# Attention in a one-core kernel: a fourth slot for the keys, the first block's operands loaded by themselves, and projection products ahead of two transposition groups

## The chip, the cores and the metric

The program runs on one core of a Trainium2 chip. A core has a matrix engine (PE in the profile; PEld is its weight load, which runs beside it), a vector engine (DVE), a scalar engine (ACT), a general engine (POOL), and a queue engine (SP) that issues nearly all transfers. The metric is the device time of one execution in microseconds (us), and lower is better.

## The reference, cut to what matters

The program computes a two-layer backbone over 1024 latent tokens with 256 context tokens ahead of them. Only the first layer's mixer, differential attention with 8 heads, is touched here; the second layer and both MLPs are computed as before.

```python
def attend(q, k, v):
    s = jnp.einsum('bqhcd,bkhcd->bhcqk', q, k).astype(jnp.float32)
    p = jax.nn.softmax(s, axis=-1)
    w = p[:, :, 0] - lam * p[:, :, 1]
    o = jnp.einsum('bhqk,bkhe->bqhe', w.astype(v.dtype), v)
    return rmsnorm(o, subln_g) * (1.0 - lambda_init)
...
q_l, k_l, v_l = jnp.split(jnp.einsum('btd,de->bte', h_lat, w_qkv), [QK_COLS, 2 * QK_COLS], axis=-1)
q_l = apply_rope(heads_qk(q_l), cos, sin) * scale
k_l = apply_rope(heads_qk(k_l), cos, sin)
```

A head has two score maps (c = 0 and 1) over 1280 keys, and its result is the first softmax less lambda times the second, times the values. Latent queries see all 1280 keys, and context queries the 256 context keys.

## The kernel before, in words

**Precision and products.** A float32 operand is held as a rounded high part and a remainder. `mm3` (L130) makes one product of three matmuls, which are the lines L132, L133 and L134 of the profile, so whole projections show up as runs of these three lines. Score matmuls are L575 (unit 0) and L581 (other units).

**Two stages.** `phase_v` (L360) normalises the tokens, computes the values of all heads and stores them in DRAM (Vd). In the last token blocks of its loop (`nb` 1, `n` from 1) it also runs `b_start` (L652), a generator that computes head 0's keys and queries, one projection group at each `n`: three for the keys, then three for the queries. Each group is scaled or rotated on ACT, DVE and POOL, split into its two parts in the 4 KB tile `self.stg` (kilobytes 12 to 16 of the region R), and stored from there to Kd or Qd. Then `phase_b` (L679) does the attention.

**Units.** `phase_b` runs 72 units, nine for each head, and then five that only finish. Unit 0 of a head (u0) has the context queries and needs only the first 256 columns of the two key maps; units u1 to u8 have 128 latent queries each against all keys. In a unit n the engines do:

- PE: the scores of this unit; where there are any, the weights-times-values products of an earlier pair of units; then three parts, each made of the transpositions of the previous unit's weight matrix (L622, L627: 4, 2 and 4 blocks of 128 x 128) and some of the eight products of a projection group for the next head. `AHEAD` says which unit has which group, and `FILLS` how the eight products are dealt to the parts: without an entry three, three and two, each behind its part's transpositions.
- DVE: `maxima` copies both score maps out of PSUM while it takes their extremes (L594), `combine` subtracts the maps (L612, L613, L615), L636 makes the low part of the first transposed part, and L529, L524, L537 and L138 serve the projection groups.
- ACT: L635 and L640 take the transposed parts out of PSUM, L604 is the exp of a score map (two in a unit), and L137 and L528 serve the groups.
- POOL: L641 and L642 split the second and third transposed part, L534 is the sine product of the rotation.

The first and the third transposed part share PSUM bank 5 in units that have a group. In the units 0, 1 and 4, 6, 8 ("late") L636 comes behind `combine` on DVE, so the first transposed part of the following unit waits for it.

**What sets the order.** In `phase_b` PE, DVE, ACT and POOL run in the order in which the code is written. SP's order is made by a scheduler, which puts a transfer where its model of the program finds it ready, and SP issues strictly in that order. A transfer that has to wait for something holds up all behind it on SP. All these transfers share one queue (q1).

**Slots.** K of a head is two tiles of 1280 columns (c = 0 and 1) in three slots of the region R1 (5 KB each, `Kr`, L687), so the second key map of the next head goes into a slot that the current head still reads, and is loaded after unit 8's scores (`load_k` behind `scores`). For head 7 it goes to the start of R. Q has two slots of 256 queries (`Qr`), V four (`Vr`). Head 0's first loads are `load_k` twice, `load_q` twice and `load_v`, at the start of `phase_b` (L853 to L857).

Of the kernel before, what the change touches and what calls it, by code (L numbers as in the profile page):

```python
# [6 lines left out]
F32 = mybir.dt.float32  # L7
F32R = mybir.dt.float32r
# [5 lines left out]
KB = 256  # L14
# [47 lines left out]
class Ring:  # L62
# [3 lines left out]
    def next(self):  # L66
        self.i += 1
        return self.items[self.i % len(self.items)]


class Prog:
# [288 lines left out]
    def phase_v(self):  # L360
# [7 lines left out]
        wr = [(self.rv(51 - 8 * i, 2, 512), self.rv(55 - 8 * i, 2, 512)) for i in range(4)]  # L368
        wt = [(hi[:, j], lo[:, j]) for hi, lo in wr for j in range(2)]
        wq = I["attn_w_qkv"][0].rearrange("(k p) n -> p k n", p=128)  # L370
        stg = Ring([self.rv(x, 2, 512) for x in (19, 23)])

        def load(ring, nb, order=range(4)):
            raws = [ring.next() for _ in order]
            for kk, raw in zip(order, raws):
                self.dma(shaped(raw, (2, 512)), wq[:, 2 * kk : 2 * kk + 2, 2048 + 512 * nb : 2560 + 512 * nb])
            return raws

        def weights(raws, order, engs):
            for raw, kk, eng in zip(raws, order, engs):  # L380
# [23 lines left out]
        loaded = []  # L404
# [18 lines left out]
        def columns(q):  # L423
# [39 lines left out]
        for nb in range(2):  # L463
            for n, (g, i) in enumerate(tok[4 * (1 - nb) :]):
                if nb == 0 and n < 2:
                    for k in range(4 * n, 4 * n + 4):
                        feature(2, k)
                b = proj.next()
                ks = range(7, -1, -1) if (nb, n) in ((0, 5), (1, 0)) else range(8)
                for k in ks:  # L470
                    product(b, g, i, k, ks)
                if nb == 0 and n == 1:
                    raws += load(Ring([self.fv(0, 1024), self.fv(4, 1024)]), 1, (1, 0))
                elif nb == 0 and n == 5:
                    weights(raws, range(3, -1, -1), [None] * 4)
                    self.lam_setup()
                out(b, nb, g, i)
                if nb and n == 1:
                    queries = self.b_start()
                if nb and n:  # L480
                    next(queries, None)
                self.step(6 if nb and n else 7)
        self.drain()
        for _ in queries:
# [82 lines left out]

    def scores(self, u, Q, K):
        mm = self.nc.tensor.matmul
        if u == 0:  # L570
            for t in range(2):
                for c in range(2):
                    o = self.PS[:, 512 * t + 256 * c : 512 * t + 256 * c + 256]
                    for r in range(2):
                        mm(o, Q[:, c, r, 128 * t : 128 * t + 128], K[c][:, 0:256], start=r == 0, stop=r == 1)  # L575
            return
        qs = slice(128 * ((u - 1) % 2), 128 * ((u - 1) % 2) + 128)
        for c in range(2):
            for k0, k1 in (((0, 512), (512, 1024), (1024, 1280)), ((0, 256), (256, 768), (768, 1280)))[c]:
                for r in range(2):  # L580
                    mm(self.PS[:, 1280 * c + k0 : 1280 * c + k1], Q[:, c, r, qs], K[c][:, k0:k1], start=r == 0, stop=r == 1)  # L581

# [64 lines left out]


    AHEAD = {0: (1, 0), 1: (1, 2), 2: (1, 1), 3: (0, 2), 5: (0, 0), 7: (0, 1)}
    FILLS = {1: (0, 0, 4, 8), 3: (0, 4, 8, 8)}  # L650

    def b_start(self):  # L652

# [22 lines left out]
        for f in post:  # L676
            f()

    def phase_b(self):  # L679
        nc, mm = self.nc, self.nc.tensor.matmul  # L680
        p0 = Ring([self.view(self.F1, 5 * i, (1280,)) for i in range(2)])
# [2 lines left out]
        o = self.fv(6, 256)  # L684
        sq = self.adat
        self.raw = Ring([self.wv(0, 1024)])
        Kr = Ring([self.view(self.R1, 5 * i, (1280,)) for i in range(3)])  # L687
        Vr = Ring([self.rv(36 + 5 * i, 10, 128) for i in range(3)] + [self.view(self.R1, 15, (10, 128))])
        Qr = Ring([self.rv(51 + 4 * i, 2, 2, 256) for i in range(2)])
        self.wT = self.rv(16, 10, 256), self.rv(26, 10, 256)  # L690
        pb = self.bank(6)
        loaded = {}

        def load_k(h, c):
            K = loaded[h, "k", c] = self.rv(0, 1280) if (h, c) == (7, 1) else Kr.next()
            for k0, k1 in ((0, 256), (256, 1280)):
                self.dma(K[:, k0:k1].bitcast(F32), self.Kd[h % 2, c, :, k0:k1])

        def load_v(h):
            V = loaded[h, "v"] = Vr.next(), Vr.next()  # L700
# [1 line left out]
                self.dma(V[j].bitcast(F32), self.Vd[h, j])  # L702

        def load_q(h, pair):
            Q = Qr.next()
            cols = slice(256 * pair, 256 * pair + 256)
            self.dma(Q[:, :, 0].bitcast(F32), self.Qd[h % 2, :, :, cols].rearrange("c r n -> r c n"))
            for hl in range(2):
                self.dma(Q[64 * hl : 64 * hl + 64, :, 1].bitcast(F32),
                         self.Qd[h % 2, :, 64 - 64 * hl : 128 - 64 * hl, cols].rearrange("c r n -> r c n"))  # L710
            loaded[h, pair] = Q

        def values(h, pair):
            V = loaded[h, "v"]
# [137 lines left out]
        self.qb = Ring([self.bank(7)])  # L852
        load_k(0, 0)  # L853
        load_k(0, 1)
        load_q(0, 0)
        load_q(0, 1)
        load_v(0)  # L857
        units = [(h, u) for h in range(8) for u in range(9)]
# [16 lines left out]
        with self.manual():  # L875
            for n in range(72 + 5):
                h, u = units[n] if n < 72 else (8, 9)
                front = n < 72
                groups = []
# [5 lines left out]
                if h == 7 and u > 5:  # L885
                    load6(u)
                if front:
                    K = loaded[h, 'k', 0], loaded[h, 'k', 1]
# [1580 lines left out]
    def run(self):  # L2469
        tc = self.tc  # L2470
        pool = lambda name, **kw: tc.tile_pool(name=name, bufs=1, **kw)
        with pool("cst") as self.cst, pool("psp", space=bass.MemoryType.PSUM) as psp, \
# [20 lines left out]
            self.misc = Ring([self.bank(i) for i in range(6, 8)])  # L2493

            with pool("r0") as rp, pool("fc") as cp:
                self.R, self.F = rp.tile([128, 59 * KB], F32R, name="R0"), cp.tile([128, 8 * KB], F32, name="FC")
                with pool("f0") as fp, pool("sp") as sp:
                    self.F0, self.SP = fp.tile([128, 41 * KB], F32, name="F0"), sp.tile([128, 12 * KB], F32, name="SP")
                    self.f0 = lambda off, *dims: self.view(self.F0, off, dims)
                    self.setup()  # L2500
                    self.phase_v()
                with pool("r1") as rp, pool("f1") as fp:
                    self.R1, self.F1 = rp.tile([128, 20 * KB], F32R, name="R1"), fp.tile([128, int(25.5 * KB)], F32, name="F1")
# [75 lines left out]
```

## Time and profile before

| | us |
|---|---|
| median of the runs | 2849.98 (2846.97 to 2850.45, 3 runs) |
| span of the profiled execution, core 0 | 2849.8 |
| `phase_b`, from its first scores to the last | 222.7 to 845.5 |
| one head, from one head's first transposition to the next's | about 78.3 |

The profile page gives busy time by engine, the costliest groups of instructions and the chain of waits; the trace behind it answers in finer views: who waited for whom, a list of instructions in order of time (start, duration, engine, line, operation, tiles, count, and in brackets the engine's idle time before it and what ended it), and tables by stretch of time. Times in these views count from the span's start. The span is within 0.2 us of the median, so sums against the span may be read as sums against the median.

### The profile page before, as it was taken

What the parts mean: (1) busy time and instruction counts of PE and PEld (TensorE: products, weight loads), DVE (VectorE), ACT (ScalarE), POOL (GpSimd) and SP (SyncE); (2) the same over time, 40 slices, a digit from 0 to 9 for tenths busy, and PEclk for the clock granted to TensorE, in tenths of its full rate; (3) what the DMA queues carried; (4) which work ended last, traced back from release to release, by engine and by line L of the source; (5) the groups of instructions that cost most, each with busy time, mean ns of one, the idle gap of its engine ahead of it and who ended that gap; (6) DMA issues with size and microseconds to landing.
All of it is one profiled execution on the core that took longest, in us unless ns stands there. A gap on an engine that the chain in (4) does not pass through costs nothing.

```text
span 2849.8 us, 43385 instructions
## 1 busy us (share of the span) xinstructions
PE 2723.3 (96%) x15229; PEld 2283.1 (80%) x15229; DVE 2019.8 (71%) x2984; ACT 1369.5 (48%) x2583; POOL 1037.2 (36%) x901
## 2 busy tenths in 40 slices
PE   6999999999999999999999999789999999999999
PEld 4688888888877887778877878688887778888887
DVE  6357788888873667767698878799543597668466
ACT  3425555565653753333444445487444633344443
POOL 3314676766663600000030013688121143336414
PEclk9999999999999999999999999899999999999999
DMA  9955555655825359886799878579742144476544
GB/s 279 319 172 188 152 173 172 177 171 171 256 91 182 128 179 316 294 302 216 249 312 310 272 238 263 169 228 306 235 154 98 66 163 160 155 246 227 167 131 142
DMA packets 414823, 586.30 MB, mean 206 GB/s; under 512 B 41870, under 2 KB 260236, under 8 KB 411404
## 3 DMA queue, kind: packets, MB, share of 16 engines
q1 hardware_dynamic: 414604, 583.52, 63.5%
q8 instruction: 120, 1.97, 0.3%
q14 instruction: 99, 0.81, 0.1%
HBM read 396.38 MB, written 182.82 MB: 203 GB/s over the span
## 4 chain that ended last, share of the span: by engine, by line
PE 76%; DVE 9%; DMA 5%; issue 4%; POOL 3%; ACT 2%; SPq 1%; DVEq 0%; ACTq 0%; POOLq 0%
PE PS L132 21%; PE PS L134 20%; PE PS L133 20%; PE PS L581 4%; PE PS L627 2%; PE PS L1928 2%; PE PS L1963 2%; DMA FU<-in_mlp_w 1%; DMA Ta<-FU 1%; PE PS L202 1%; DVE R L138 1%; SPq L80 1%; DVE F L615 1%; ACT F L604 1%; DVE H L138 1%
## 5 line engine op out<-in xcount | busy, mean ns | idle before, releaser
L132 PE MATMUL PS<-H 128*128 128x512 f32 x1072 | 420.6, 393 | 2.7 <-ACT H L137 1.7
L134 PE MATMUL PS<-H 128*128 128x512 f32 x1072 | 417.5, 390 | 2.8 <-DVE H L138 1.5
L133 PE MATMUL PS<-H 128*128 128x512 f32 x1072 | 417.7, 390 | 0.0
L132 PE MATMUL PS<-H,R 128*128 128x512 f32 (+1 forms) x828 | 308.0, 374 | 4.3 <-ACT R L137 2.0
L133 PE MATMUL PS<-H,R 128*128 128x512 f32 (+1 forms) x828 | 298.6, 361 | 0.0
L134 PE MATMUL PS<-H,R 128*128 128x512 f32 (+1 forms) x828 | 298.0, 361 | 0.0
L132 PEld LDWEIGHTS PS<-H 128*128 128x128 f32 x1072 | 201.2, 188 | 50.5 <-issue 6.4
L134 PEld LDWEIGHTS PS<-H 128*128 128x128 f32 x1072 | 201.2, 188 | 46.1 <-DVE H L138 2.3
L133 PEld LDWEIGHTS PS<-H 128*128 128x128 f32 x1072 | 201.3, 188 | 40.6
L604 ACT ACTIVATE F<-F,stat 128x1280 f32<-128x1280 f32 x128 | 174.3, 1362 | 106.6 <-DVE F L594 106.5
L137 ACT ACTIVATE H<-U 128x640 fp32r<-128x640 f32 x216 | 131.9, 674 | 172.6 <-PE PS L133 138.3
L137 ACT ACTIVATE R<-W 128x512 fp32r<-128x512 f32 (+1 forms) x184 | 128.7, 707 | 174.1 <-PE PS L133 101.5
L132 PE MATMUL PS<-R,H 128*128 128x512 f32 x520 | 208.0, 401 | 3.3 <-ACT H L137 3.3
L134 PE MATMUL PS<-R,H 128*128 128x512 f32 x520 | 205.0, 396 | 1.8 <-DVE H L138 1.8
L133 PE MATMUL PS<-R,H 128*128 128x512 f32 x520 | 204.5, 394 | 0.0
L138 DVE TENSOR_TENSOR H<-U,H 128x640 fp32r<-128x640 f32 x216 | 165.1, 797 | 50.6 <-ACT H L137 49.6
L138 DVE TENSOR_TENSOR H<-W,H 128x512 fp32r<-128x512 f32 (+1 forms) x137 | 125.2, 924 | 102.8 <-ACT H L137 102.1
L594 DVE TENSOR_SCALAR_CACHE_REDUCE F<-PS 128x1280 f32<-128x1280 f32 x128 | 185.2, 1483 | 9.3 <-PE PS L581 9.1
L137 ACT ACTIVATE H<-W 128x512 fp32r<-128x512 f32 (+2 forms) x158 | 95.4, 613 | 188.7 <-PE PS L133 116.8
L132 PEld LDWEIGHTS PS<-H,R 128*128 128x128 f32 x828 | 157.6, 191 | 30.2 <-issue 4.1
L134 PEld LDWEIGHTS PS<-H,R 128*128 128x128 f32 x828 | 157.0, 190 | 25.2 <-issue 0.8
L641 POOL TENSOR_SCALAR R<-F 128x256 fp32r<-128x256 f32 (+1 forms) x128 | 126.5, 989 | 136.0 <-ACT F L640 122.4
(534 smaller groups left out, 6860.0 us busy)
## 6 DMA issues: line engine op xcount, KB each, us to landing
W<-in_mlp_w SPq DMA_DIRECT2D x176, 256.0 KB
U<-Aa SPq DMA_DIRECT2D x108, 320.0 KB
Aa<-FU SPq DMA_DIRECT2D x91, 320.0 KB
Ad<-F SPq DMA_DIRECT2D x112, 256.0 KB
W<-Ad SPq DMA_DIRECT2D x112, 256.0 KB
FU<-in_mlp_w SPq DMA_DIRECT2D x32, 512.0 KB
Ta<-FU SPq DMA_DIRECT2D x16, 1024.0 KB
U<-in_ada_w SPq DMA_DIRECT2D x32, 512.0 KB
```

The costliest lines, as they stand in the source:

```text
L132: mm(out, ah, bh, start=first, stop=False, **kw)
L133: mm(out, ah, bl, start=False, stop=False, **kw)
L134: mm(out, al, bh, start=False, stop=last, **kw)
L137: self.nc.scalar.activation(hi, src, AF.Copy)
L138: (lo_eng or self.nc.vector).tensor_tensor(lo, src, hi.bitcast(F32), ALU.subtract)
L581: mm(self.PS[:, 1280 * c + k0 : 1280 * c + k1], Q[:, c, r, qs], K[c][:, k0:k1], start=r == 0, stop=r == 1)
L594: ts(p[c], self.PS[:, 1280 * c : 1280 * c + 1280], 1.0, None, ALU.mult, ALU.min, accum_out=sm[:, c : c + 1])
L604: nc.scalar.activation(p[c], p[c], AF.Exp, bias=sm[:, c : c + 1], scale=-1.0, accum_out=sn[:, 0:1] if c else s0[:, u + 1 : u + 2])
L627: self.nc.tensor.transpose(tb[:, 128 * (kt - k0) : 128 * (kt - k0) + 128], w[:, 128 * kt : 128 * kt + 128], self.ident)
L641: nc.gpsimd.tensor_scalar(hi, t, 1.0, 0.0, ALU.mult, ALU.add)
L1928: mm(b[:, o : o + 160], X[:, d, i, 64 * j : 64 * j + 128], U[:, 4 * n + i, cols], start=True, stop=True)
L1963: mm(o, cs[d][n % 2][j][:, i], W[:, d, i], start=False, stop=d == 1 and j == 1)
```

## The change

R grows from 59 to 60 KB a partition and R1 from 20 to 25 KB. The values' weights and staging tiles in R move up by 1 KB, which leaves kilobytes 16 to 20 free in the last part of `phase_v`.

```diff
-        stg = Ring([self.rv(x, 2, 512) for x in (19, 23)])
+        stg = Ring([self.rv(x, 2, 512) for x in (20, 24)])
...
+                if nb and n == 7:
+                    self.first = self.rv(16, 2, 2, 256), [self.rv(12 + c, 256) for c in range(2)]
+                    self.load_q(self.first[0], 0, 0)
+                    for c, K in enumerate(self.first[1]):
+                        self.dma(K.bitcast(F32), self.Kd[0, c, :, 0:256])
...
-    FILLS = {1: (0, 0, 4, 8), 3: (0, 4, 8, 8)}
+    FILLS = {0: (3, 5, 7, 8), 1: (0, 0, 4, 8), 3: (0, 4, 8, 8), 5: (2, 4, 6, 8)}
...
-        Kr = Ring([self.view(self.R1, 5 * i, (1280,)) for i in range(3)])
-        Vr = Ring([self.rv(36 + 5 * i, 10, 128) for i in range(3)] + [self.view(self.R1, 15, (10, 128))])
+        Kr = Ring([self.view(self.R1, 5 * i, (1280,)) for i in range(4)])
+        Vr = Ring([self.rv(36 + 5 * i, 10, 128) for i in range(3)] + [self.view(self.R1, 20, (10, 128))])
...
-            K = loaded[h, "k", c] = self.rv(0, 1280) if (h, c) == (7, 1) else Kr.next()
...
-        load_q(0, 0)
         load_q(0, 1)
         load_v(0)
...
-                    Q = loaded[h, pair]
+                    Q, K = self.first if n == 0 else (loaded[h, pair], (loaded[h, 'k', 0], loaded[h, 'k', 1]))
...
                     if u == 5 and h < 7:
                         load_v(h + 1)
                         load_k(h + 1, 0)
+                        load_k(h + 1, 1)
+                    if u == 7 and h < 7:
+                        load_q(h + 1, 0)
...
                     if u == 8 and h < 7:
-                        load_k(h + 1, 1)
-                        load_q(h + 1, 0)
                         load_q(h + 1, 1)
...
                     fills = [groups[0][0][a[i] : a[i + 1]] for i in range(3)]
+                    for f in groups[0][0][: a[0]]:
+                        f()
```

So unit 0 of head 0 reads its queries and the first 256 key columns from tiles of their own, loaded at `n` = 7 of `phase_v`; `load_q` becomes a method with the same three transfers for a pair. The two small key tiles lie in kilobytes 12 to 14 of R, which are part of `self.stg`. A first number above 0 in `FILLS` is the number of products that run ahead of the first transpositions: three in u0, two in u5.

**SP's queue at the start of `phase_b`.** Before, twelve rows on SP from the last of head 0's full key loads (R_1850 is R1, R_110 is R, `x2` is two transfers; `Vd<-R` stores values, `Qd<-R` stores queries from `self.stg`, `R<-Qd` loads queries, `R<-Vd` loads values; unit 0 needs the keys and the first three `R<-Qd`):

```order
L80 DMA R_1850<-Kd 128x1024
L80 DMA Vd<-R_110 128x4x128
L80 DMA R_110<-Qd 128x2x256
L80 DMA Vd<-R_110 128x4x128
L80 DMA R_110<-Qd 64x2x256 x2
L80 DMA Qd<-R_110 64x2x512 x2
L80 DMA R_110<-Qd 128x2x256
L80 DMA R_110<-Qd 64x2x256
L80 DMA Vd<-R_110 128x4x128
L80 DMA R_110<-Qd 64x2x256
L80 DMA Vd<-R_110 128x4x128
L80 DMA R_110<-Vd 128x1280 x3
```

After, the same place (R_1855 is R1):

```order
L80 DMA R_110<-Qd 64x2x256
L80 DMA Vd<-R_110 128x4x128
L80 DMA R_110<-Qd 128x2x256
L80 DMA R_110<-Qd 64x2x256
L80 DMA Qd<-R_110 64x2x512 x2
L80 DMA R_110<-Vd 128x1280 x2
L80 DMA R_110<-Qd 128x2x256
L80 DMA Vd<-R_110 128x4x128 x2
L80 DMA R_110<-Qd 64x2x256 x2
L80 DMA R_110<-Vd 128x1280
L80 DMA R_1855<-Vd 128x1280
L80 DMA R_110<-Kd 128x256 x2
```

The first queries are no longer here (their three loads stand 8 rows ahead, behind an earlier group's `FC<-FC`), the loads shown are those of the second and third pair of queries, and the two small key loads of unit 0, the last row, stand behind all four loads of the values.

**SP's queue at the end of a head.** Before, in unit 8 of head 0 (`FC<-FC` is the four-way swap of a group that has just left PSUM):

```order
L80 DMA Qd<-R_110 64x2x512 x2
L80 DMA FC<-FC 32x512 x4
L80 DMA R_1850<-Kd 128x256
L80 DMA R_1850<-Kd 128x1024
L80 DMA R_110<-Qd 128x2x256
L80 DMA R_110<-Qd 64x2x256 x2
```

After, in unit 4 of head 0, right behind the store of the keys that they read:

```order
L80 DMA Kd<-R_110 64x2x512 x2
L80 DMA R_1855<-Kd 128x1024 x2
L80 DMA FC<-FC 32x512 x4
L80 DMA R_110<-Qd 128x2x256
L80 DMA R_110<-Qd 64x2x256 x2
```

The second key map's two loads left the end of the head; each now follows the first map's load of the same width, some four to six units earlier.

**PE in unit 5.** Before, from the last scores of u5 in head 1:

```order
L581 MATMUL PS<-R_1850,R_110 128x512 x4
L627 MATMUL PS<-ident,F_1851 128x128 x4
L132 MATMUL PS<-H,R_110 128x512
L133 MATMUL PS<-H,R_110 128x512
L134 MATMUL PS<-H,R_110 128x512
```

After (L586 is the scores' line now, L632 the transpositions'):

```order
L586 MATMUL PS<-R_1855,R_110 128x512 x4
L132 MATMUL PS<-H,R_110 128x512
L133 MATMUL PS<-H,R_110 128x512
L134 MATMUL PS<-H,R_110 128x512
L132 MATMUL PS<-H,R_110 128x512
L133 MATMUL PS<-H,R_110 128x512
L134 MATMUL PS<-H,R_110 128x512
L632 MATMUL PS<-ident,F_1856 128x128 x4
```

Six matmuls, two products, moved from behind the first four transpositions to ahead of them; in u0 it is nine. Between the first and the third group of transpositions stand four products in place of six.

More of the change, by code (lines that the diff above doesn't have):

```diff
@@ L367, in phase_v @@
         proj = Ring([self.bank(i) for i in range(4)])
-        wr = [(self.rv(51 - 8 * i, 2, 512), self.rv(55 - 8 * i, 2, 512)) for i in range(4)]
+        wr = [(self.rv(52 - 8 * i, 2, 512), self.rv(56 - 8 * i, 2, 512)) for i in range(4)]
         wt = [(hi[:, j], lo[:, j]) for hi, lo in wr for j in range(2)]
         wq = I["attn_w_qkv"][0].rearrange("(k p) n -> p k n", p=128)
-        stg = Ring([self.rv(x, 2, 512) for x in (19, 23)])
+        stg = Ring([self.rv(x, 2, 512) for x in (20, 24)])
         def load(ring, nb, order=range(4)):
@@ L677, in b_start, with load_q @@
             f()
+    def load_q(self, Q, h, pair):
+        cols = slice(256 * pair, 256 * pair + 256)
+        self.dma(Q[:, :, 0].bitcast(F32), self.Qd[h % 2, :, :, cols].rearrange("c r n -> r c n"))
+        for hl in range(2):
+            self.dma(Q[64 * hl : 64 * hl + 64, :, 1].bitcast(F32),
+                     self.Qd[h % 2, :, 64 - 64 * hl : 128 - 64 * hl, cols].rearrange("c r n -> r c n"))
     def phase_b(self):
@@ L694, in load_k, with load_cols @@
         def load_k(h, c):
-            K = loaded[h, "k", c] = self.rv(0, 1280) if (h, c) == (7, 1) else Kr.next()
-            for k0, k1 in ((0, 256), (256, 1280)):
-                self.dma(K[:, k0:k1].bitcast(F32), self.Kd[h % 2, c, :, k0:k1])
+            loaded[h, "k", c] = Kr.next()
+            load_cols(h, c, 0, 256)
+            load_cols(h, c, 256, 1280)
+        def load_cols(h, c, k0, k1):
+            self.dma(loaded[h, "k", c][:, k0:k1].bitcast(F32), self.Kd[h % 2, c, :, k0:k1])
         def load_v(h):
@@ L704, in load_q @@
         def load_q(h, pair):
[L705 to L711, printed above, removed]
+            loaded[h, pair] = Qr.next()
+            self.load_q(loaded[h, pair], h, pair)
         def values(h, pair):
@@ L887, in phase_b @@
                 if front:
-                    K = loaded[h, 'k', 0], loaded[h, 'k', 1]
                     pair = (u + 1) // 2
-                    Q = loaded[h, pair]
+                    Q, K = self.first if n == 0 else (loaded[h, pair], (loaded[h, 'k', 0], loaded[h, 'k', 1]))
                     s0 = hst[:, 0, h]
@@ L2495, in run @@
             with pool("r0") as rp, pool("fc") as cp:
-                self.R, self.F = rp.tile([128, 59 * KB], F32R, name="R0"), cp.tile([128, 8 * KB], F32, name="FC")
+                self.R, self.F = rp.tile([128, 60 * KB], F32R, name="R0"), cp.tile([128, 8 * KB], F32, name="FC")
                 with pool("f0") as fp, pool("sp") as sp:
@@ L2502, in run @@
                 with pool("r1") as rp, pool("f1") as fp:
-                    self.R1, self.F1 = rp.tile([128, 20 * KB], F32R, name="R1"), fp.tile([128, int(25.5 * KB)], F32, name="F1")
+                    self.R1, self.F1 = rp.tile([128, 25 * KB], F32R, name="R1"), fp.tile([128, int(25.5 * KB)], F32, name="F1")
                     self.phase_b()
```

## The prediction

> **What bounds the kernel now.** I read the page's first part, then tables by stretch of time, then each engine's waits over five of the eight heads, and last lists in order of time at the places that the change touches. In the tables by stretch the columns are start and end, length, busy time (and instructions) of PE, PEld, DVE, ACT and POOL, granted clock, DMA share and GB/s.
>
> ```profile
> PE 2723.3 (96%) x15229; PEld 2283.1 (80%) x15229; DVE 2019.8 (71%) x2984; ACT 1369.5 (48%) x2583; POOL 1037.2 (36%) x901
> 215.00:232.00 17.00, 11.86 (x50) 9.64 (x49) 5.28 (x17) 3.41 (x11) 0.83 (x1) 0.90 1.05 353
> 540.00:620.00 80.00, 76.41 (x490) 67.97 (x489) 67.28 (x103) 47.74 (x97) 54.88 (x53) 1.00 0.60 175
> ```
>
> PE is nearly full, but the shares differ by stage. At the start of `phase_b` (215 to 232) the transfers are saturated (1.05) and PE stands a third of the time. Inside a head (540 to 620) PE and DVE are both close to full, so time that PE gains is worth something only where DVE and ACT can follow. The waits from 295 to 691 (total, times, longest) say how much there is:
>
> ```profile
> PE PS L575 <- DMA R<-Kd: 10.0, 6, 2.2
> PE PS L627 <- DVE R L636: 9.2, 11, 1.2
> DVE stat L612 <- ACT F L604: 43.2, 35, 2.0
> DVE F L594 <- PE PS L581: 1.9, 7, 0.5
> ```
>
> PE loses 10.0 at the heads' first scores to the second key map, and 9.2 to transpositions that wait for L636: 19.2 in all, the ceiling on what the heads can give. DVE waits for PE only 1.9, against 43.2 for ACT's exps: the softmax chain runs nearly as long as PE does.
>
> **Part 1, the first loads: a cost S.** The list by time (start, duration, engine, line; in brackets the idle time before and its cause), PE first, the last row from a later head's start, then SP; then the chain's step for a query load, the sizes of the transfers issued from 213 to 235, and two stretches of time:
>
> ```profile
> 222.71 0.35 PE L575 MATMUL PS<-R,R 128*128 128x256 f32 x1 [4.17 <-issue]
> 224.04 1.83 PE L575 MATMUL PS<-R,R 128*128 128x256 f32 x7 [0.97 <-DMA R<-Qd]
> 451.10 0.98 PE L575 MATMUL PS<-R,R 128*128 128x256 f32 x6 [1.62 <-DMA R<-Kd]
> ```
>
> ```profile
> 219.32 1.31 SPq L80 DMA_DIRECT2D Qd<-R  x2
> 232.58 2.48 SPq L80 DMA_DIRECT2D FC<-FC  x4
> 448.82 1.02 SPq L80 DMA_DIRECT2D R<-Kd  x2
> ```
>
> ```profile
> 218.37 5.54 DMA R<-Qd
> R<-Vd SPq DMA_DIRECT2D x4, 640.0 KB
> R<-Kd SPq DMA_DIRECT2D x2, 128.0 KB
> R<-Qd SPq DMA_DIRECT2D x3, 256.0 KB
> FC<-FC SPq DMA_DIRECT2D x4, 64.0 KB
> 231.00:234.00 3.00, 3.00 (x16) 2.50 (x16) 1.39 (x2) 1.12 (x2) 0.89 (x1) 1.00 1.00 404
> 234.00:237.00 3.00, 3.00 (x27) 2.97 (x26) 2.81 (x5) 2.34 (x4) 0.41 (x1) 1.00 0.72 188
> ```
>
> Before, PE's last projection ends at 218.54 (222.71 less the 4.17 idle) and unit 0's scores get going at 224.04, when the last query load has landed. After the change the queries are issued ahead of the burst, but the keys come later, for two reasons. Their tiles are part of `self.stg`, so they must wait until the query store issued at 219.32 has read it; and in SP's order they are the last of the burst, behind four value loads of 640 KB. The queue is full, so they land when the burst ends. Before, it ends inside 234 to 237: 188 GB/s over 3 us are 564 KB, and the stretch before it moved 404 GB/s, so those take 1.4 us and the end is at 235.4. The four 64 KB swaps issued at 232.58 are in it but not ahead of the keys: 256 KB, 0.6 us, 234.75. Off go the first queries, one transfer of 256 KB and two of half the partitions, 512 KB together, on come two key loads of 128 KB: 256 KB less, 0.6, so 234.1. With about 0.9 us from the last data to PE (an estimate, less than half of the 2.28 that a key load takes from issue, 448.82, to the scores, 451.10, at a head's start) the scores start at 235.0 in place of 224.04: **S = 11.0**. Bounds: 9.5 if they land at 233.5, ahead of the last value packets; 12.5 if the swaps get in front. If the order of issue did not hold back the keys, only the store would: its second half issued at 220.0, landed 5.54 later (as long as the query load at 218.37) at 225.5, plus those 2.28: 227.8, S = 3.8.
>
> The row at 218.37, 5.54 us for a load behind others while the queue's share was 1.05, is what this rests on. [...]
>
> **Part 2, the heads: a gain G.** PE's first transpositions of three heads, then the first unit that has products ahead and whose L636 is late (u2 of the same head, whose lead was made in u0): PE, DVE and ACT.
>
> ```profile
> 374.51 0.66 PE L627 MATMUL PS<-ident,F 128*128 128x128 f32 x4 [0.71 <-DVE R L636]
> 452.83 1.11 PE L627 MATMUL PS<-ident,F 128*128 128x128 f32 x4 [0.75 <-DVE R L636]
> 532.41 0.66 PE L627 MATMUL PS<-ident,F 128*128 128x128 f32 x4 [0.19 <-DVE R L636]
> 392.09 0.68 DVE L636 TENSOR_TENSOR R<-PS,R 128x512 fp32r<-128x512 f32 x1
> 393.90 0.60 PE L627 MATMUL PS<-ident,F 128*128 128x128 f32 x4
> 394.43 0.08 DVE L594 DVE_READ_ACCUMULATOR F<-PS 128x1 f32 x1
> 394.54 0.60 ACT L635 ACTIVATE R<-PS 128x512 fp32r<-128x512 f32 x1 [3.05 <-PE PS L627]
> 395.03 1.36 ACT L604 ACTIVATE F<-F,stat 128x1280 f32<-128x1280 f32 x1
> 396.83 0.39 ACT L640 ACTIVATE F<-PS 128x256 f32<-128x256 f32 x1 [0.35 <-PE PS L627]
> 397.11 1.36 ACT L604 ACTIVATE F<-F,stat 128x1280 f32<-128x1280 f32 x1
> ```
>
> The key wait (1.62 at 451.10) goes: the load now stands by u4's store, and nothing between it and the scores holds it up. What is late next is L636 again. In u0 three products now run where PE stood 0.71 for L636; with the key wait of 1.62 that is up to 2.33 by which PE is ahead when it gets to u2. There the first transpositions (393.90) can't go before L636, 392.09 + 0.68 = 392.77: 1.13 of the lead is used, the rest becomes a new wait. What the 1.13 is worth is decided on ACT: L635 waited 3.05 for these transpositions, so the first exp may start when the maximum is read (394.43 + 0.08 = 394.51, not 395.03), and the second then at 396.24 in place of 397.11, since L640's 0.35 wait falls too. DVE's `combine` waits for that exp, so **0.9** per head goes on.
>
> ```profile
> 418.43 0.66 PE L627 MATMUL PS<-ident,F 128*128 128x128 f32 x4 [1.20 <-DVE R L636]
> 422.14 0.68 DVE L636 TENSOR_TENSOR R<-PS,R 128x512 fp32r<-128x512 f32 x1
> 423.31 0.60 PE L627 MATMUL PS<-ident,F 128*128 128x128 f32 x4
> 432.23 0.60 ACT L635 ACTIVATE R<-PS 128x512 fp32r<-128x512 f32 x1 [0.55 <-PE PS L627]
> 438.64 1.77 DVE L537 TENSOR_TENSOR FC<-FC 128x512 f32<-128x512 f32 x1 [0.84 <-POOL FC L534]
> ```
>
> In u5 two products fill the 1.20 wait. But the third transpositions share bank 5 with the first, so they wait until L636 has read it: 422.14 + 0.68 = 422.82, against 423.31 now. PE gains **0.5**, and the other 0.7 of that wait comes back before the third transpositions. In u6 ACT waits on PE (0.55) and through POOL DVE does (0.84), so the 0.5 goes on. Six heads (1 to 6) by 1.4: 8.4. Heads 0 and 7 I take at nothing: head 0's lead at the start is S itself, head 7 has no groups.
>
> ```profile
> 370.20:373.60 3.40, 1.72 (x15) 1.50 (x13) 2.20 (x4) 3.02 (x7) 1.79 (x2) 1.00 0.68 167
> 448.70:452.10 3.40, 1.76 (x14) 1.36 (x11) 2.28 (x4) 2.84 (x7) 1.96 (x2) 1.00 0.69 209
> 452.10:455.50 3.40, 2.67 (x9) 2.28 (x10) 2.74 (x11) 1.52 (x5) 3.23 (x5) 0.51 0.99 324
> ```
>
> One head, after the key wait at 451.10, ran 3.4 us at a clock of 0.51, and that head took 532.41 − 452.83 = 79.6, against 452.83 − 374.51 = 78.3 for the one before. Without the wait I expect no dip: 1.3. So **G = 8.4 + 1.3 = 9.7**, with bounds 3.0 (only u5's 0.5) and 20.5 (all 19.2 and the dip). The first two rows have almost the same busy time, yet only the second was followed by half clock. [...]
>
> **At nothing:** the moved tiles (addresses alone); the query load from u8 to u7 (it stands at the same place of SP's order); head 7's other key slot. The second map's loads stand behind a store, where SP already waits (from 205 to 850):
>
> ```profile
> SPq L80 <- DMA Kd<-R: 12.5, 10, 1.9
> SPq L80 <- ACT FC L528: 24.6, 7, 3.9
> ```
>
> That is 1.25 each, hidden because SP next waits for ACT's L528 anyway; if that cover fails, a swap is about 1 us late in each of seven heads, and L537 with it: 7 us, an unlikely edge.
>
> **Sum:** span 2849.8 (the median within 0.2) + 11.0 − 9.7 = 2851.1, **2851**.
>
> **Rivals.** A is this forecast: loss and gain nearly cancel; own range 2845 to 2857 by S's 9.5 to 12.5 and G between 5 and 14. B: every PE wait in the heads turns into time, 2849.8 + 11.0 − 19.2 − 1.3 = 2840.3. For it: PE is the fullest engine. Against: DVE waits for PE only 1.9. C, the other side: at u2 DVE and ACT don't take up the lead, because the chain from one exp to the next binds there; then G is u5's 3.0, and 2849.8 + 11.0 − 3.0 = 2857.8. It decides from 0.9 us a head downwards: below a G of 5.3 the start outweighs the heads by more than 5.7. For it: DVE's 43.2 on exps. Against: ACT's 3.05 idle before L635. D: the keys aren't held behind the values, as the change means to have it, S = 3.8: 2843.9. Against it: the 5.54.
>
> **How the numbers follow.** A 0.58, B 0.15, C 0.20, D 0.07. A measurement tells about 0.2%, 5.7 us. B, two thirds of D and 0.03 of A make faster 0.23; C but 0.01 and 0.08 of A make slower 0.27; the rest is 0.50. The range goes from B's edge, 2839, to 2859, C with a start 1.2 dearer.
>
> **What would show it.** PE idle of about 16 us before unit 0's scores, released by a key load: right if near 235; near 228 means D. No wait on R<-Kd at later heads. New waits of about 1 us on L636 at u2's first and u5's third transpositions; a head of about 76.9 instead of 78.3, with no half clock. Heads still at 78 mean C, heads at 75 mean B. Wrong altogether would be a key load at a head's start that is late in its new place.

## The result, and the profile after

The changed kernel is slower: median 2860.1 us of 20 runs (2853.78 to 2870.35) against 2850.8 of 20 runs before; ratio 1.0031, 95% interval 1.0023 to 1.0039, which is 6.6 to 11.1 us. The prediction was 2851, with a range to 2859. The profiled execution is one of the changed kernel's faster ones (2855.4, its span 2853.6).

Below are the page's first line of the changed kernel, then PE around unit 0's first scores, SP's rows that lead to them, and PE's and DVE's waits from 310 to 702, five heads as in the table shown of before. All lines moved: scores are L580 (u0) and L586, transpositions L632, the low part L641, the copies L595 (u0) and L599, `combine` L617, L618 and L620.

```profile
PE 2724.5 (95%) x15229; PEld 2283.0 (80%) x15229; DVE 2020.3 (71%) x2984; ACT 1367.7 (48%) x2583; POOL 1033.4 (36%) x901
```

```profile
237.68 2.05 PE L580 MATMUL PS<-R 128*128 128x256 f32 x8 [16.68 <-issue]
```

```profile
221.74 1.37 SPq L80 DMA_DIRECT2D Qd<-R  x2
229.19 1.11 SPq L80 DMA_DIRECT2D R<-Vd  x2
231.04 0.98 SPq L80 DMA_DIRECT2D R<-Kd  x2
```

```profile
PE PS L132 <- ACT F L645: 5.5, 5, 1.1
PE PS L632 <- DVE R L641: 3.8, 5, 0.8
PE PS L133 <- DVE R L641: 3.2, 4, 0.8
DVE stat L617 <- ACT F L609: 39.7, 35, 1.6
```

No work was added: every engine's busy time is that of before within 4 us. PE stands 16.68 us before the first scores, where it stood 4.17 and 0.97. In the heads the wait on R<-Kd (10.0) is gone, and the transpositions' wait for the low part (L636 before, L641 now) fell from 9.2 to 3.8. But 3.2 + 5.5 = 8.7 stand there in waits that the list of before does not have, so more than half of the 15.4 that went came back under another name.

To see where time is won and lost, the lists by time of two kernels are laid beside each other: DVE's work is the same in both, so the start of the same copy says how late the program is at that place. The table gives, against the trace of before, the start of the first copy of head 0 (225.06 there), of a copy in unit 0 of head 7 (766.80) and of the first copy of head 7's u3 (794.85). What `phase_v` had already lost or won (read from a DVE copy at 183.95 in the trace of before; from -1.8 to +2.8 over the traces, from -0.1 to +2.5 in the change's own three) is taken off.

| kernel | first copy | head 7 u0 | head 7 u3 |
|---|---|---|---|
| the change, first trace | +11.4 | +6.5 | +4.9 |
| again | +11.8 | +6.4 | +9.4 |
| again2 | +10.5 | +4.4 | +4.4 |
| nofirst | +0.6 | -4.7 | -2.5 |
| firstonly | +10.7 | +10.6 | +10.6 |
| qonly | -5.5 | -10.0 | -7.9 |
| q_nofill | -5.6 | -6.8 | -6.8 |
| q_fill0 | -4.9 | -9.7 | -6.1 |
| q_fill5 | -4.8 | -1.3 | +1.0 |
| keysact | +11.9 | +6.7 | +9.0 |
| keysaway | -6.0 | -12.5 | -9.7 |
| aw | +13.9 | +7.9 | +8.9 |
| qw | -5.0 | -12.3 | -11.3 |
| after7 | +11.5 | +6.5 | +6.9 |
| away7 | -6.0 | -12.4 | -10.9 |

Three steps are to be seen in the change's own three traces: a start that costs 10.5 to 11.8 (up to 13.9 in `aw`, whose edit lies in head 7 alone), heads that give back some 5 to 6, and head 7, which goes from -1.5 to +3.0. Read from head 1's first copy on (296.06 in the trace of before), the heads are steadier: they give 6.3, 5.7 and 6.1 in the change's traces and 6.2 in `nofirst` and `keysaway`. What is missing from that in the table is head 0, where the change's three lose 1.4, 0.4 and 0.0. Behind `phase_b` the traces drift from that of before by -5.9 to +2.2 us, the repeats of one kernel too (-3.6, +2.2 and -4.8 for the change).

### The profile page after: what moved, and what is told of

It reads as the page before. It is cut to its first block, busy times and chain, and to the rows that moved or that the text cites. A ratio compares the mean times of both kernels' runs of the same rounds, so it can differ in the third digit from the quotient of the medians.

```text
span 2853.6 us, 43375 instructions
## 1 busy us (share of the span) xinstructions
PE 2724.5 (95%) x15229; PEld 2283.0 (80%) x15229; DVE 2020.3 (71%) x2984; ACT 1367.7 (48%) x2583; POOL 1033.4 (36%) x901
## 5 line engine op out<-in xcount | busy, mean ns | idle before, releaser
L599 DVE TENSOR_SCALAR_CACHE_REDUCE F<-PS 128x1280 f32<-128x1280 f32 x128 | 185.1, 1483 | 6.4 <-PE PS L586 6.2
L132 PEld LDWEIGHTS PS<-H,R 128*128 128x128 f32 x828 | 157.6, 191 | 37.5 <-ACT F L645 8.2
L134 PEld LDWEIGHTS PS<-H,R 128*128 128x128 f32 x828 | 157.1, 190 | 25.5 <-issue 0.8
L133 PEld LDWEIGHTS PS<-H,R 128*128 128x128 f32 x828 | 157.7, 190 | 19.6
```

Of the source, the lines that this page charges most:

```text
L132: mm(out, ah, bh, start=first, stop=False, **kw)
L133: mm(out, ah, bl, start=False, stop=False, **kw)
L134: mm(out, al, bh, start=False, stop=last, **kw)
L599: ts(p[c], self.PS[:, 1280 * c : 1280 * c + 1280], 1.0, None, ALU.mult, ALU.min, accum_out=sm[:, c : c + 1])
```

## The experiments

**The parts by themselves.** `again` and `again2` are the change unaltered. `nofirst` takes the first loads back, `firstonly` has them alone (three slots, loads and `FILLS` as before), and `qonly` keeps the early queries but reads the keys from the full tiles:

```diff
# nofirst, against the change: self.first and its loads out, and
         load_k(0, 1)
+        load_q(0, 0)
         load_q(0, 1)
# firstonly, against the change: three slots, load_k(h + 1, 1) and load_q(h + 1, 0) back in u8, and
-    FILLS = {0: (3, 5, 7, 8), 1: (0, 0, 4, 8), 3: (0, 4, 8, 8), 5: (2, 4, 6, 8)}
+    FILLS = {1: (0, 0, 4, 8), 3: (0, 4, 8, 8)}
# qonly, against the change
-                    self.first = self.rv(16, 2, 2, 256), [self.rv(12 + c, 256) for c in range(2)]
-                    self.load_q(self.first[0], 0, 0)
-                    for c, K in enumerate(self.first[1]):
-                        self.dma(K.bitcast(F32), self.Kd[0, c, :, 0:256])
+                    self.first = self.rv(16, 2, 2, 256)
+                    self.load_q(self.first, 0, 0)
...
-                    Q, K = self.first if n == 0 else (loaded[h, pair], (loaded[h, 'k', 0], loaded[h, 'k', 1]))
+                    Q, K = self.first if n == 0 else loaded[h, pair], (loaded[h, 'k', 0], loaded[h, 'k', 1])
```

> The changed kernel unaltered, for a second trace. In the first trace phase_v ends 2.45 us later than before the change (one load of W<-in_ada_w is waited for 3.65 us, not 2.22), unit 0's first scores begin 13.6 us later, phase_b ends 7.4 later, and the end of the program is only 3.8 later. Theory T1 (the extra 2.45 and the 3.6 won back behind phase_b are arrivals of transfers that differ from run to run): here the first scores begin about 11 us later than the before trace's and the wait in the first 80 us is again near 2.2. Rival T2 (the moved tiles or the order of transfers cost phase_v 2.45 each time): the 2.45 is here too.

> The change without its first loads: four key slots, the query load in unit 7 and the products ahead stay; unit 0 of head 0 reads the full tiles, loaded in the order of before. T1: the heads alone are worth 6.4 (heads 0 to 6 in the trace of the change) and head 7's unit 3 another 1.5, so 2850.8 - 7.9 = 2843. T2 (a cost of about 4 us outside phase_b that comes with the moved tiles): 2847. If the heads give nothing by themselves (the gain was PE catching up after a late start): 2851.

> The first loads alone: unit 0's queries and first 256 key columns in tiles of their own, loaded where the change loads them; three key slots, later loads and products as before. T1: first scores 11.2 later and 1.4 more of half clock behind them, 2850.8 + 12.6 = 2863. If a late start is partly caught up in the heads: 2856 to 2860.

> The change, but unit 0 takes its keys from the full tiles (loaded ahead of the values) and only its queries from the early tile. T1: no key load behind the values or behind the last query store; the second key map's first columns should land some 3 us ahead of the time at which the last query load landed before the change, so first scores 3 to 4 us earlier than before, and with the heads' 7.9 the time is 2839. If the queue's order is not what held the keys back in the change: no better than the change, 2860.

Measured: `nofirst` 0.9995 (0.9985 to 1.0004), `firstonly` 1.0047 (1.0030 to 1.0064), `qonly` 0.9961 (0.9948 to 0.9975; 2840.0). The first loads alone are a loss of 8.5 to 18 us, and taking only their key tiles away turns the change into a gain. `again` and `again2` gave 2863.0 and 2852.7, one run each; their `phase_v` is 0.1 earlier and 1.5 later than before, so the first trace's 2.45 is scatter, as T1 had it. T1's 2843 for `nofirst` missed: its heads gave 5.3 in the trace, but head 7 took 2.2 of it back and the start 0.6, and what the runs show in the end, 0.3 less than before, is within noise of nothing.

**Why the keys are late.** `keysact` has ACT issue the two key loads, on a queue of its own; `keysaway` puts their tiles outside the staging tile; `vheld` holds a value load of head 1 back by laying the first queries in its place.

```diff
# keysact
-                        self.dma(K.bitcast(F32), self.Kd[0, c, :, 0:256])
+                        self.nc.scalar.dma_start(out=K.bitcast(F32), in_=self.Kd[0, c, :, 0:256])
# keysaway (R 62 KB, F0 40.5 KB)
-... [self.rv(12 + c, 256) for c in range(2)]
+... [self.rv(60 + c, 256) for c in range(2)]
# vheld
-self.first = self.rv(16, 2, 2, 256), ...
+self.first = self.rv(46, 2, 2, 256), ...
```

> The change, with one thing different: unit 0's two key loads are issued by ACT and so go on a queue of their own; tiles and everything on the other engines as in the change. Theory T1 (the keys are late because they are last in one queue, behind four value loads; the store that they must wait for has landed by 228 in the trace of the change): with a queue of their own they are issued at about 228.3, land near 231, and the first scores begin some 6 us earlier than the 237.7 of the change (less its 2.45 of late start); time 2860 - 6 = 2854. Rival (the transfers' total rate is the limit, whichever queue): scores no earlier, 2860. Rival (the wait for the store is all of it): scores above 2 us after the store, the same 231; this one can't be told from T1 by the time, but by the issue of the loads.

> The change, with unit 0's two key tiles at kilobytes 60 and 61 of R (grown to 62), outside the staging tile; all else as in the change. Theory P (the place of the tiles is the whole cause of the late start: inside the staging tile they can't be loaded before the last query store has read it, and so come last in the burst): the loads go out long before the burst, first scores follow the last projection within 0.5 us, no half clock behind them, and the time is that of the early queries with full key tiles, 2840, 0.996 of before. Rival (small tiles of their own cost something else, in the burst or behind it): between 2845 and 2860.

> The change, with the first queries' tile at kilobytes 46 to 50 of R, which is where half of head 1's values go: that value load can't start before unit 0's scores, and one value load of 640 KB and two stores of 256 KB then stand behind the key loads and not ahead of them. The key tiles are still in the staging tile. Theory P with bytes in flight (the loads wait for what is ahead of them in the burst, at about 0.41 MB a us, whichever queue they are on): 1.15 MB less ahead, so PE idles 16.7 - 2.8 = 14 us before the first scores, if the queries, loaded later here, are not the last. If the store's landing alone held them: 16.7 as in the change.

`keysact` did not start earlier. Its transfers from 225 to 240 (rate, queue, issue with the time to landing), then ACT's row and PE's:

```profile
GB/s 434 401 429 423 437 437 396 423 322 314 306 339 351 348 347 362 413 430 317 314 396 382 437 440 363 423 366 341 186 49 0 0 0 0 0 0 0 0 0 0
q10 hardware_dynamic: 288, 0.26, 5.1%
R<-Kd ACTq DMA_DIRECT2D x2, 128.0 KB, 6.4
```

```profile
229.95 0.82 ACTq L486 DMA_DIRECT2D R<-Kd  x2
236.46 2.05 PE L580 MATMUL PS<-R 128*128 128x256 f32 x8 [17.14 <-issue]
```

The 0.26 MB went over q10, with nothing of its own ahead, and still took 6.4 us from issue to landing; PE stood 17.14. Its time is the change's, 1.0038 (1.0023 to 1.0054). The rate row, 40 slices of 0.375 us from 225 on, falls to nothing at 236.25, which is where PE starts (236.46): here the loads land as the whole burst ends. The packets of each microsecond say the same: q10 moved none before 233, then 13, 88 and 181 in the three stretches from there, while q1 went from 93 to 63 and 31. So in this trace it is not their place in one queue that costs the time: on a queue of their own they still landed only when the burst had drained.

That is only the part behind the issue, though. PE had been idle for 10.6 us (from 219.32) when ACT issued the two loads at 229.95, and ACT's work ahead of them had ended at 220.01. By the code they had the store out of the staging tile to wait for; the trace names no cause. An estimate from these rows: with the 2.28 us of a key load at a head's start and no burst, the scores would start at 232.2, which is 7.4 later than before once the 0.8 of `phase_v` is taken off. So most of the late start may lie ahead of the issue.

`keysaway` did start early: in its list by time PE's first scores have no wait ahead of them, and the same for `qonly`, with 0.23:

```profile
219.84 1.12 PE L580 MATMUL PS<-R 128*128 128x256 f32 x8
```

```profile
219.28 0.98 PE L578 MATMUL PS<-R,R 128*128 128x256 f32 x6 [0.23 <-DMA R<-Kd]
```

It ran at 0.9967 (0.9956 to 0.9979; 2839.5). Same tiles, same sizes, another two kilobytes: theory P holds. The wait for the store with no burst behind it was not run apart; the 7.4 above is all there is on it. `vheld` tells nothing on it: its queries land in a tile of the values' weights that the last two token blocks' products still read, so those values are others, PE waits 7.84 us for the loads already in `phase_v` and then 6.99 for the keys.

**What the heads give.** `q_nofill`, `q_fill0` and `q_fill5` are `qonly` with the two new entries of `FILLS` out, or only the one for u0 or u5 in.

```diff
# q_nofill; q_fill0 adds 0: (3, 5, 7, 8), q_fill5 adds 5: (2, 4, 6, 8)
-    FILLS = {0: (3, 5, 7, 8), 1: (0, 0, 4, 8), 3: (0, 4, 8, 8), 5: (2, 4, 6, 8)}
+    FILLS = {1: (0, 0, 4, 8), 3: (0, 4, 8, 8)}
```

> Early queries, keys from the full tiles, four slots, but the products ahead of the transpositions in u0 and u5 taken back. Theory F (the prediction's working with its places corrected): in the trace the key waits are gone and L627-type waits on L636 in u0 and u5 are back near 0.7 and 1.2; a head is shorter than before only by what the key wait carried into u3 (0.38), and the u5 step of 0.36 is gone; against the early queries with products about 2 us slower (2842). Rival (the products ahead carry all of the heads' gain, the fourth slot none): heads as before, 78.3 each, 2846.

> Early queries, keys from the full tiles, four slots, and three products ahead in u0 but none in u5. Theory F (at u2 the values products, which need L636's low part too, stand ahead of the transpositions, so the lead is worth 0.37 and not 0.9): in the trace DVE's first copy of u3 comes 0.37 earlier in each of heads 2, 4, 5 and 6 against the trace of before, and nothing is gained behind u5. The prediction's own figure: 0.9.

> Early queries, keys from the full tiles, four slots, and two products ahead in u5 but none in u0. Theory F: 0.36 in each head from u5 to u6, none from u2 to u3, so about half of what the two places give together. Prediction's figure for u5: 0.5.

`q_nofill` measured 0.9992 (0.9979 to 1.0005), 2848.5 where 2842 was expected. In its trace heads 1 to 5 give 1.2, all of it in head 3, the one with half clock in the trace of before (0.51 for 3.4 us): the fourth slot alone gives nothing else there (head 0 gives 0.9 more and head 6 loses 1.0). At head 7's u3 it is only 1.1 behind `qonly`, while its median is 8.5 above; its traced execution is the fastest of its ten, and where the others lose their time is not shown. `q_fill0`: from u2 to u3 DVE's first copy gains 0.37, 0.38, 0.39 and 0.36 in heads 2, 4, 5 and 6, and nothing behind u5, as theory F had it. `q_fill5`: the u5 step is there (0.34 to 0.39 in heads 1, 2, 3, 5 and 6, none in head 4), but in heads 2, 5 and 6 units 1 to 3 lose 1.6 to 2.8 us that no other trace loses; in head 2 a DVE instruction of the projection group (L527) waits 0.76 for ACT there. What causes it is not shown; it says that u5's products without u0's are not a safe half.

**Head 7.** In `aw` and `qw` the output projection's second weight pair goes to kilobytes 0 to 8 of R; in `after7` and `away7` POOL's part of its split comes one unit later.

```diff
# aw, qw
-... for t, x in ((self.R1, 0), (self.R, 8), (self.R, 36))]
+... for t, x in ((self.R1, 0), (self.R, 0), (self.R, 36))]
# after7, away7: wsplit6 does ACT's half, wlow6 POOL's
+            if u == 1:
+                wlow6(1)
+                wlow6(2)
```

> The change, with the second weight pair of the output projection written to kilobytes 0 to 8 of R in head 7, not to 8 to 16, whose upper part is the staging tile of the projection groups. Theory H (in head 7's unit 2 POOL's split of these weights waits for the last query store to land; landing a little earlier in the change, POOL begins just ahead of DVE's combine, and DVE's L620 takes 3.5 in place of 1.6 us; PE then waits 3.2 for L641): POOL's split begins right behind L647 with no 5 us wait, L620 takes under 2.1, and head 7's unit 3 is not later against the trace of before than unit 2 is; 2860.1 - 3 = 2857, and the runs lie in one group. Rival (the step has another cause, or POOL's split collides with another DVE operation): 2860, with unit 3 still some 3 us later in part of the runs.

> Early queries with the keys from the full tiles, and the weight pair at kilobytes 0 to 8 of R. Theories T1 and H together: the early queries' 0.9961 of before (2840) and the 3 us of head 7: 2837, 0.995. If H is wrong: 2840.

> The change, with POOL's split of the second weight pair of the output projection placed one unit later in head 7 (the end of unit 1, ahead of the third pair's; ACT's half stays where it is), so that it can't begin beside unit 1's combine. Theory H (the change's lost time in head 7 is DVE standing behind POOL's split, when the last query store lands just ahead of the combine): DVE's combine in that unit takes 0.22 and 1.6 to 2.0, the first copy of unit 3 is about 2.5 us earlier than in the repeat of the change, and the median is 2860 - 2.5 = 2857.5. Rival (the lost time comes back at the two splits in a row, behind which PE waits): no step in unit 1 but the same in unit 2 or 3, 2860.

> The key tiles outside the staging tile, and the same move of POOL's split as in the run beside this one. Theory H: 2839.5 - 2.5 = 2837, 0.9958 of before. Rival: 2839.5.

> The changed kernel unaltered, a third trace. Theory H: either POOL's split of 128x1024 in head 7's unit 1 begins ahead of DVE's combine, which then takes 2 us longer, with unit 3 some 3 us later against the trace of before than unit 1, or it begins behind it, and unit 3 is 1.5 us earlier, as in the first trace. Anything between speaks against H.

(In `aw`'s expectation "unit 2" is the second of the head, u1.) `aw` 1.0032 (1.0021 to 1.0044), `qw` 0.9972 (0.9961 to 0.9984), 2843.5: no gain where 3 us were expected. POOL's wait is gone, but the split now runs beside the operations ahead and costs 1.0 there. `after7` 1.0024 (1.0015 to 1.0033), 2856.9, 10 of 11 runs within 2854.2 to 2858.6: 3.2 below the change and near theory H's 2857.5, though the two intervals overlap; head 7 costs 0.4. `away7` 0.9959 (0.9947 to 0.9972), 2840.1: the rival's number, not H's 2837; in its trace head 7 still costs 1.5. `again2` fell between: POOL began behind `combine`, and head 7 cost 0.0, not -1.5; so the first trace's -1.5 had another cause beside. As `after7` has one trace, and two of the change's three do without the loss too, H rests on the rows shown below more than on these medians.

## Why the prediction was wrong

**The start** was right: 11.0 predicted, 10.5 to 11.8 in the change's three traces. Its reason was half right. In the change's first trace the keys were issued at 231.04 and the burst ended near 237.4, just ahead of PE's 237.68, at about the rate that was read (392 GB/s from 226 to 236, against 404). But that the order of issue in one queue is what holds them back was the author's assumption, which no run shows: in `keysact`, on a queue of their own, they landed at the end of the burst too (6.4 us from issue, 6.5 in the change). Rival D's 3.8, in turn, had the store land at 225.5, while the loads in `keysact` went out at 229.95. (The lower bound of S left out the 0.9 to PE: a landing at 233.5 gives 10.4, not 9.5.) What the sum has no term for is the clock behind the idle time; here are the trace of before, from 224, and of the change, from 237.6 (the column before the last two is the granted clock):

```profile
224.00:228.00 4.00, 3.96 (x15) 3.56 (x16) 1.98 (x11) 2.10 (x8) 0.00 (x0) 0.64 1.12 379
228.00:232.00 4.00, 4.00 (x20) 3.28 (x19) 1.22 (x4) 0.08 (x1) 0.00 (x0) 1.00 1.01 416
```

```profile
237.60:241.60 4.00, 3.92 (x13) 3.53 (x14) 1.76 (x10) 1.90 (x7) 0.00 (x0) 0.50 0.01 2
241.60:245.60 4.00, 4.00 (x15) 3.15 (x13) 1.44 (x5) 0.21 (x2) 0.00 (x0) 0.74 0.00 0
```

Of the clock 0.36 is missing for 4 us before, and 0.50 and 0.26 after: (0.76 - 0.36) x 4 = 1.6 us more. Between `again2`'s copies the same place cost nothing more than before, so this term is between 0 and 1.6. The length of the idle time doesn't settle it: `firstonly` was idle for 16.02 us and has 0.65 and then 1.00, `nofirst` for 5.85 and has 0.50 and 0.85. The term stands in the table between the first copy and head 7, where it takes from the heads' gain.

**The heads** gave 4.9 to 6.1 in the change's traces, 5.3 in `nofirst` and 6.5 in `keysaway`, not 9.7. The half clock of head 3 (0.51 for 3.4 us before) went with its wait, as predicted, and gave 1.2 of the 1.3 that the sum counts for it: PE's first transpositions of heads 2 and 3 stand 77.57 apart,

```profile
389.08 0.60 PE L632 MATMUL PS<-ident,F 128*128 128x128 f32 x4
466.65 0.60 PE L632 MATMUL PS<-ident,F 128*128 128x128 f32 x4
```

and where the clock had been 0.51 the table by stretch has 1.00:

```profile
465.90:469.30 3.40, 3.40 (x19) 2.81 (x19) 2.09 (x10) 1.63 (x6) 3.32 (x5) 1.00 0.74 226
```

The step that failed is u2's 0.9. These are two of PE's rows of before at u2 of head 2, the first of six matmuls that run up to the transpositions at 393.90, then DVE's and PE's rows of the changed kernel there:

```profile
393.19 0.28 PE L132 MATMUL PS<-R 128*128 128x256 f32 x1
393.30 0.28 PE L133 MATMUL PS<-R 128*128 128x256 f32 x1
```

```profile
405.99 0.68 DVE L641 TENSOR_TENSOR R<-PS,R 128x512 fp32r<-128x512 f32 x1
406.72 0.39 PE L133 MATMUL PS<-R 128*128 128x256 f32 x1 [0.79 <-DVE R L641]
407.42 0.60 PE L632 MATMUL PS<-ident,F 128*128 128x128 f32 x4
406.93 1.47 DVE L599 TENSOR_SCALAR_CACHE_REDUCE F<-PS 128x1280 f32<-128x1280 f32 x1
416.28 1.48 DVE L599 TENSOR_SCALAR_CACHE_REDUCE F<-PS 128x1280 f32<-128x1280 f32 x1
```

The prediction let the transpositions go when L636 (here L641) ends. But in u2 the values products stand between, and their second matmul reads that low part itself: it starts at 406.72, when L641 is done, and the transpositions 0.70 later. Of the 1.13 that was counted, 0.7 was this chain. From u2's copy to u3's it is 416.28 - 406.93 = 9.35, against 402.75 - 393.02 = 9.73 before:

```profile
393.02 1.48 DVE L594 TENSOR_SCALAR_CACHE_REDUCE F<-PS 128x1280 f32<-128x1280 f32 x1
402.75 1.48 DVE L594 TENSOR_SCALAR_CACHE_REDUCE F<-PS 128x1280 f32<-128x1280 f32 x1
```

0.38, and heads 4, 5 and 6 give the same within 0.02; head 1 gives 0.95, and why is not shown. u5 went as told, with its new wait before the third transpositions, and gave 0.36 for 0.5:

```profile
435.67 0.68 DVE L641 TENSOR_TENSOR R<-PS,R 128x512 fp32r<-128x512 f32 x1
436.41 0.66 PE L632 MATMUL PS<-ident,F 128*128 128x128 f32 x4 [0.78 <-DVE R L641]
```

Over heads 1 to 6 of the change's first trace u2 gives 2.8 where the prediction had 5.4, u5 2.3 for 3.0, and the clock of head 3 1.2 for 1.3: 6.3 in all, less what head 0 loses ahead of them.

**Head 7** was taken at nothing, and here is a term that the sum lacks. The split of a weight pair (128x1024) writes kilobytes 8 to 16 of R, of which POOL's half is `self.stg`, so POOL waits for the last query store, and comes free beside unit 1's `combine`. POOL's, DVE's and PE's rows there, before and in `again`:

```profile
783.07 1.55 DVE L615 SCALAR_TENSOR_TENSOR F<-F,stat 128x1280 f32<-128x1280 f32 x1
783.22 3.62 POOL L138 TENSOR_TENSOR R<-W,R 128x1024 fp32r<-128x1024 f32 x1 [5.98 <-DVE stat L613]
```

```profile
789.07 2.37 POOL L138 TENSOR_TENSOR R<-W,R 128x1024 fp32r<-128x1024 f32 x1 [5.30 <-ACT W L137]
789.26 3.53 DVE L620 SCALAR_TENSOR_TENSOR F<-F,stat 128x1280 f32<-128x1280 f32 x1
793.45 0.58 PE L133 MATMUL PS<-R 128*128 128x256 f32 x1 [3.18 <-DVE R L641]
```

In these rows the one that began first ran at its own length (1.55 for DVE, 2.37 for POOL), and the other took, within 0.2 us, what was left of the first and then its own length: 3.62 for POOL (1.40 + 2.37), 3.53 for DVE (2.18 + 1.55). With POOL 0.19 us ahead DVE loses 2 us, PE waits 3.18 for the low part, and u3 is 3.0 later. Before, POOL was only 0.15 behind. Of the eleven traces with four slots and this split in its place POOL was first in eight (`again`, `nofirst`, `qonly`, `keysact`, `keysaway`, `vheld`, `q_fill0`, `q_fill5`; +2.1 to +3.7), of the two with three slots in none. That this coincidence costs time is shown by these rows, and head 7 is 2.1 to 3.7 dearer in the eight traces that have it. It stands in one of the change's three traces, so how many of its runs pay it, and whether some runs of before do, is not; and why the store lands earlier with four slots (SP's order differs around it by two H<-on loads) is only read from the order.

The step of the sum that failed is thus G: 9.7 became 4.9 to 6.1, mostly by the values products that stand ahead at u2, and the sum had no term for head 7, -1.5 to +3.0 in the change's traces. With 11.2 at the start (the middle of the three) that is 2849.8 + 11.2 - 5.5 + 1.7 = 2857.2, or 7.4 more than before, where 6.6 to 11.1 more were measured (another 1.0 of the miss is that 20 runs of before have their median at 2850.8, not at 2849.8). The 1.7 is an estimate: the change's times fall into nine up to 2857.9 and eleven from 2860.1 on, and it takes `again`'s 3.0 for the eleven. `again` ran at 2863.0 and the two traces without this loss at 2855.4 and 2852.7, but that the upper group is the one with POOL ahead is not shown. What remains may lie in the drift behind `phase_b`, which the traces don't settle. Of the rivals C came nearest in time, 2857.8, and not by its mechanism: the lead at u2 was taken up, as far as it was free.

The fastest version is the change without the key tiles in the staging tile: `qonly` 0.9961, `keysaway` 0.9967 and `away7` 0.9959 of before, which can't be told from each other.

## What to carry to other kernels

A tile that is to be loaded early is better kept off the bytes of a buffer whose last store is late: here the loads went out 10.6 us after PE had run dry (`keysact`) and landed as the burst ended, and two kilobytes elsewhere were worth some 18 us. Before a freed wait is counted as won, read the whole row of work behind it: the next instruction that needed the same operand took 0.7 of u2's 1.13 back. And where a DVE and a POOL instruction come free within a few tenths of a microsecond (0.15 and 0.19 in head 7), an edit far away can swap them; here that cost DVE 2 us.

## What the runs showed of the hardware

A DVE instruction on one column took nearly as long as the POOL instruction on 1024 that ran beside it: 2.20 us against 2.34. The rows of `keysaway` in head 7, where POOL is 0.16 ahead:

```profile
771.63 2.34 POOL L138 TENSOR_TENSOR R<-W,R 128x1024 fp32r<-128x1024 f32 x1 [5.41 <-ACT F L609]
771.79 2.20 DVE L618 SCALAR_TENSOR_TENSOR stat<-FC,stat,lamc 128x1 f32<-128x1 f32 x1
```

L618 on 128x1 takes 0.22 in `after7`, and here 2.20, to 773.99, which is POOL's end (773.97) within 0.02. In six of the eight traces with POOL ahead this one-column instruction took 2.19 to 2.33 (`nofirst`, `keysact`, `keysaway`, `vheld`, `q_fill0`, `q_fill5`). In the other two, `again` and `qonly`, it had begun 0.06 and 0.18 ahead of POOL and took 0.22, and the subtraction behind it took 3.53 and 3.63 in place of 1.55. What ties the two engines together there is not shown.

A queue of its own, started from another engine, didn't bring two loads of 128 KB past the burst on the first: 6.4 us to landing, none of it moved in the first 3 us, against the 2.28 from issue to scores of a key load at a head's start.
